# One RWKV step on Trainium2: the decay in a step's last operation, outputs behind the next step's first products, row halves in turn

## The chip, the cores and the metric

The kernel runs on one core of a Trainium2 chip. The core has a matrix engine (PE, which reads its stationary operand by a weight load, PEld), a vector engine (DVE), a scalar engine (ACT), a general engine (POOL) and a queue that issues transfers (SP); each works through its own instructions in order and waits for the others by semaphores. The metric is the device time of one execution in microseconds (us), as the median of several runs.

## The reference, cut to what matters

One layer of a hybrid network for 512 latent tokens and 128 context tokens, all float32:

```python
proj = (x * (1 + sc1) + sh1) @ p["w_in"]              # one input projection
att = _attend(q_nope, q_rope, k_nope, k_rope, v)      # 8 heads, low-rank keys and values
rw, s_fwd, s_bwd = _rwkv_mixer(proj[..., OFF_RW:], ...)  # 16 heads x 64, one scan per direction
x = _post_norm(x, g1, _merge(att, rw, p), ...)        # output projection, norm
x = _post_norm(x, g2, _swiglu(x * (1 + sc2) + sh2, p), ...)   # feed-forward part

def step(S, inp):                                     # the RWKV scan, token by token
    r_t, w_t, k_t, v_t, kk_t, a_t = inp
    sa = jnp.einsum("bhvk,bhk->bhv", S, -kk_t)
    S = S * w_t[:, :, None, :] + sa[..., None] * (kk_t * a_t)[:, :, None, :] + v_t[..., None] * k_t[:, :, None, :]
    return S, jnp.einsum("bhvk,bhk->bhv", S, r_t)
```

The scan runs forwards and backwards over the tokens; `w_t` is the decay of the state.

## The kernel before, in words

The first 1540 us hold three jobs. The **main** job multiplies the modulated input with 33 tiles of `w_in` (each 16 x 6 products of 320 columns, written `acc<-xh,whi` and the like in the profile: a float32 product is split into three of a faster type). The **RWKV** job goes through 8 pairs of heads. The **attention** job follows once the main job is done. From 1540 us on come the output projection and the feed-forward part, with one product after the other from streamed weights; the change leaves these lines alone.

RWKV takes the tokens in chunks of 64, so a pair has two halves (`j`), each with five steps (`e`) in both directions at once. A half has these stages, each a generator that gives way with `yield HOP[...]`:

- `rwkv_decays`: four small products with `lw` (128 rows), each corrected by one over 64 rows (`m<-xl,lw`), then the decays `ld`, `D` and `dc`.
- `rwkv_prep` and `rwkv_grams`: 20 products `m<-pr,nk` with 64 rows each, for the two heads of the pair in the two halves of the rows; their masks are put on while they are taken from PSUM into `pr`, `mab` and `mrb`.
- `inverse`: `mab` is brought into another layout (`nd`), a triangular solve runs on DVE, and its result `tc` goes back to PE (`m<-tc,mab`). Beside it `rwkv_turned` turns the values (`sv`, `zv`) and `nk` (`bk`).
- `rwkv_chain`: the five steps, one behind the other. A step is: the first product `m<-sv,pr`, copied to `xs`; the solve `m<-xs,uf`, copied to `zv`; the update `m<-zv,bk`, from which the next state `sv` is made with the decay `dc`; and the outputs `m<-pr,sv` plus `m<-mrb,zv`, added into `y`.

The order on PE is written out when the program is built. `Jobs` keeps a clock of PE (`Tensor.now`, raised by a cost per product) and always takes the job of the best rank that is ready; RWKV has the best rank, the main and the attention job the last. A job that gives way is ready again after the time it yields (`HOP`, with one table for the stretch beside the main job and one beside attention). So these numbers say how much other work PE is given between two products that depend on each other; at run time PE waits if the data are not there. The other engines' order is made by a scheduler.

The last stretch of the main job is set by `fs`: the tiles 2 to 25 belong to the pairs 0 to 7, three each, 26 to 29 are the queries, 30 and 31 the keys and values, 32 the rotary key; a pair's RWKV begins when its three tiles are there.

PSUM has three banks for small results (`mps`, the tile `m`) and two double banks (`acc`). In attention, `kslot` gives out 12 buffers: four hold the compressed keys and values all along, two the rotary key (`krh`, `krl`), the others keys and values of the heads in turn. The lower part of the rotary key is multiplied for one head of a pair in one half of the rows (`acc<-krl,qx`, 64 rows).

Of the kernel before, what the change touches and what calls it, by code (L numbers as in the profile page):

```python
# [15 lines left out]
P = 128  # L16
# [11 lines left out]
C = 64  # L28
# [18 lines left out]
for _n, _w in (("ident", 128), ("gmask", 128), ("lmask", 32), ("par", 2), ("blk", 128), ("cen", 128), ("blk2", 2), ("sel", 2),  # L47
# [22 lines left out]
HOPS = ({"load": 3.73, "pow": 3.84, "kk": 1.18, "dec": 0.92, "prep": 1.68, "vr": 2.17, "tv": 0.36, "bk": 0.36, "gram": 0.36,  # L70
         "inv": 14.4, "d32": 1.2, "d32b": 1.92, "d64": 1.44, "d64b": 1.44, "x": 0.48, "s": 0.6, "y": 0.0, "p": 1.06,
# [3 lines left out]
         "inv": 16.13, "d32": 1.51, "d32b": 1.96, "d64": 1.3, "d64b": 1.44, "x": 0.61, "s": 0.6, "y": 0.0, "p": 1.08,  # L75
# [20 lines left out]
class Tensor:  # L96
# [5 lines left out]
    def matmul(self, out, lhsT, rhs, start, stop):  # L102
# [8 lines left out]
        self.now += t / 2400.0  # L111
# [46 lines left out]
def step_kernel(ctx: ExitStack, tc: tile.TileContext, a: dict, o: dict, upto: int = 99, npairs: int = NPAIR, dbg=None):  # L158
# [397 lines left out]
    def inverse(mab):  # L556
# [5 lines left out]
        for b in range(4):  # L562
            pr = slice(32 * b, 32 * b + 32)
            co = 32 * (b % 2)
            A.copy(nd[pr, :].rearrange("p (t c q) -> p c q t", c=16, q=2)[:, :NCH],  # L565
                   mab[pr, :, co: co + 32].rearrange("p c (q t) -> p c q t", q=2))
# [143 lines left out]
    def rwkv_decays(i, j, sh):  # L710
# [3 lines left out]
        for d in range(2):  # L714
            col = 8 * d + i
            for t, c0, x, r_, b in ((ld, 0, xw, slice(0, 64), w0_h), (ta, 256, xa, slice(64, 128), a0_h)):
                ps = mps()
                w = lw[:, c0 + d * P: c0 + d * P + P]
# [4 lines left out]
                yield HOP["dec"]  # L723
# [43 lines left out]
    def rwkv_turned(i, j, sh, u):  # L767
# [6 lines left out]
        for d in range(2):  # L774
# [6 lines left out]
            for h in range(2):  # L781
                A.copy(sv_[hrow(h), es, h, :], ch(ps[hrow(h), :HN]))
                V.tensor_copy(zv[hrow(h), es, h, :], ch(ps[hrow(h), :HN]))
# [8 lines left out]
    def rwkv_grams(u):  # L792
# [3 lines left out]
        for e0, n in EG:  # L796
            es = slice(e0, e0 + n)
            for h in range(2):
                ps = mps()
# [9 lines left out]
                tt(V, mrb[rows(h), es], ps4[rows(h), :, 1, :],  # L809
                   con("gmask")[rows(h), C:].unsqueeze(1).broadcast_to([C, n, C]), ALU.mult)  # L810
                yield HOP["gram"]
# [7 lines left out]
    def rwkv_chain(i, j, sh, u):  # L819
# [23 lines left out]
        def outputs(c):  # L843

            ps = mps()
            for d in range(2):
                e = 5 * d + c
                ms = slice(0, C) if d == 0 else slice(None, None, -1)
                for h in range(2):
                    T.matmul(ps[rows(h), cc(d)], sv_[:, e, h, :], pr[h][:, e, 1, :][:, ms], start=True, stop=False)  # L850
                for h in range(2):
                    T.matmul(ps[rows(h), cc(d)], zv[rows(h), e, h, :], mrb[rows(h), e, :][:, ms], start=False, stop=True)
            for d in range(2):
                yc = y[:, nat(d, j)][:, cc(c if d == 0 else 4 - c)]
                if j == 0:
                    A.copy(yc, ps[:, cc(d)])
                else:
                    tt(V, yc, ps[:, cc(d)], yc, ALU.add)

        for e in range(5):  # L860
# [6 lines left out]
            yield HOP["x"]  # L867
# [7 lines left out]
            to = [AFTER[j, d][e] for d in range(2)]  # L875
            ds = [d for d in range(2) if to[d]]
# [4 lines left out]
            sd = rtile("sd", 2 * C, "xs", 2)  # L881
            n = len(ds)
            for h in range(2):
                rh = rows(h)
                es = slice(5 * ds[0] + e, 5 * ds[-1] + e + 1, 5)
                dv = slice(ds[0] * C, ds[-1] * C + C)
                s2 = sd[rh, dv].rearrange("p (d v) -> p d v", v=C)
                tt(V, s2, pn[rh, dv].rearrange("p (d v) -> p d v", v=C), sv_[rh, es, h, :], ALU.add)
# [1123 lines left out]
```

## Time and profile before

| | |
|---|---|
| median of three runs | 3558.94 us (3550.21 to 3559.14) |
| the profiled execution | 3555.39 us, of which its span 3553.6 us |
| busy share of the span | PE 95%, PEld 85%, DVE 73%, ACT 41%, POOL 28% |
| first RWKV products (`m<-pr,nk`) | 264 us |
| last state written (`out_states`) | 1524 us |
| first product of the output projection | 1555 us |
| mean granted PE clock | 0.963 |

A row of the timeline has start, duration, engine, line, operation, tiles and shape, and how many equal ones were merged (x8); in brackets how long the engine sat idle before and what released it. A product in float32 is two instructions on PE, one in the faster type is one. A row of the groups has busy time and mean duration of one, then the idle time before. Durations of PE overlap, since it is pipelined; how long PE is taken up by a row is read from the start of the row after it.

### The profile page before, as it was taken

The page shows a single profiled execution, that of the slowest core. Times are in us where ns is not written, and L with a number is a line of the kernel's source. Part 1 is how long each engine was busy: PE and PEld are TensorE (multiplying, and loading weights), DVE is VectorE, ACT ScalarE, POOL GpSimd, SP SyncE. Part 2 cuts the span into 40 slices and gives each one's busy share as a digit, 9 for nine tenths or more (in the row PEclk, how much of TensorE's full clock was granted, in tenths as well). Part 3 has the DMA queues.
Part 4 walks back from the last instruction along what each step waited for, and adds up shares of the span by engine and source line. Part 5 has one row for each costly group of instructions (what it writes and reads, how often), then busy time and mean ns, then how long its engine had stood idle before and what let it go on. Part 6 is the DMA issues. An engine that isn't in the chain of part 4 may idle for free.

```text
span 3553.6 us, 71134 instructions
## 1 busy us (share of the span) xinstructions
PE 3376.3 (95%) x27538; PEld 3022.9 (85%) x27538; DVE 2609.0 (73%) x4721; ACT 1459.1 (41%) x2987; POOL 992.5 (28%) x944
## 2 busy tenths in 40 slices
PE   8979999999999899999979999999999999999987
PEld 4667776777887678889979999999999999899886
DVE  1355676666676877667788888888888879778798
ACT  1143333433444444444554444444444444334334
POOL 0021111111111212112164444344444442122245
PEclk9988999999999999999989999999999999999997
DMA  8753444444212111066534543444434468766743
GB/s 299 236 172 120 148 150 134 157 146 144 65 58 77 50 38 37 21 203 189 164 116 131 164 134 128 140 133 128 134 128 141 133 231 288 268 238 222 244 138 106
DMA packets 289715, 529.04 MB, mean 149 GB/s; under 512 B 31008, under 2 KB 83680, under 8 KB 289376
## 3 DMA queue, kind: packets, MB, share of 16 engines
q1 hardware_dynamic: 289376, 524.49, 45.1%
q8 instruction: 216, 3.54, 0.4%
q14 instruction: 123, 1.01, 0.1%
HBM read 429.65 MB, written 93.09 MB: 147 GB/s over the span
## 4 chain that ended last, share of the span: by engine, by line
PE 55%; DVE 6%; issue 2%; DMA 2%; ACT 1%; POOL 1%; SPq 0%; ACTq 0%; DVEq 0%; POOLq 0%
PE b L112 47%; PE acc L112 3%; PE m L112 3%; DVE ql L226 1%; DMA op<-hd 1%; PE x L112 1%; DVE z L226 1%; POOL z L226 1%; PE acc L116 0%; DMA raw<-in_w_down_dram 0%; DVE z L235 0%; DVE ns L226 0%; DVE raw L226 0%; ACT nd L565 0%; DVE u L226 0%
## 5 line engine op out<-in xcount | busy, mean ns | idle before, releaser
L226 DVE TENSOR_TENSOR ql<-raw,qh 128x512 fp32r<-128x512 f32 (+1 forms) x1136 | 926.3, 830 | 263.5 <-ACT qh L1290 242.8
L1290 ACT CAST qh<-raw 128x512 fp32r<-128x512 f32 (+1 forms) x1136 | 661.1, 588 | 914.0 <-PE b L112 784.1
L226 POOL TENSOR_TENSOR raw<-raw,raw 128x512 f32<-128x512 f32 (+1 forms) x288 | 397.0, 1380 | 852.2 <-DVE ql L226 654.4
L112 PE MATMUL b<-t,qh 128*128 128x320 f32 x2816 | 622.7, 310 | 8.2 <-ACT qh L1290 7.1
L112 PE MATMUL b<-op,qh 128*128 128x320 f32 x2464 | 547.0, 315 | 18.3 <-DMA op<-hd 18.0
L112 PEld LDWEIGHTS b<-t,qh 128*128 128x128 f32 x2816 | 472.6, 189 | 9.6 <-ACT qh L1290 8.1
L112 PE MATMUL b<-p,qh 128*128 128x320 f32 x2112 | 468.4, 311 | 0.0
L112 PE MATMUL b<-t,ql 128*128 128x320 f32 x1408 | 435.8, 310 | 5.8 <-DVE ql L226 5.8
L112 PEld LDWEIGHTS b<-op,qh 128*128 128x128 f32 x2464 | 418.2, 192 | 24.3 <-issue 11.7
L112 PE MATMUL b<-op,ql 128*128 128x320 f32 x1232 | 375.2, 317 | 19.7 <-DVE ql L226 19.5
L112 PEld LDWEIGHTS b<-p,qh 128*128 128x128 f32 x2112 | 355.8, 189 | 0.1
L112 PE MATMUL b<-p,ql 128*128 128x320 f32 x1056 | 328.9, 312 | 8.0 <-DVE ql L226 8.0
L112 PEld LDWEIGHTS b<-t,ql 128*128 128x128 f32 x1408 | 264.9, 188 | 8.0 <-DVE ql L226 8.0
L112 PEld LDWEIGHTS b<-op,ql 128*128 128x128 f32 x1232 | 233.1, 192 | 27.5 <-DVE ql L226 27.2
L112 PE MATMUL acc<-xh,whi 128*128 128x320 f32 x928 | 239.8, 341 | 0.3 <-DVE vS L1145 0.2
L112 PE MATMUL acc<-xl,whi 128*128 128x320 f32 x928 | 237.3, 338 | 0.0
L112 PE MATMUL b<-mh,qh 128*128 128x320 f32 x1024 | 231.0, 315 | 6.2 <-ACT qh L1290 6.1
L112 PE MATMUL acc<-xh,wlo 128*128 128x320 f32 x928 | 235.6, 336 | 0.8 <-DVE wlo L226 0.8
L226 DVE TENSOR_TENSOR raw<-raw,raw 128x512 f32<-128x512 f32 (+1 forms) x288 | 216.5, 764 | 12.5 <-POOL raw L226 10.6
L112 PEld LDWEIGHTS b<-p,ql 128*128 128x128 f32 x1056 | 199.6, 189 | 10.6 <-DVE ql L226 10.6
L263 ACT CAST whi<-raw 128x512 fp32r<-128x512 f32 (+1 forms) x156 | 94.8, 608 | 255.9 <-PE acc L112 167.1
L226 DVE TENSOR_TENSOR wlo<-raw,whi 128x512 fp32r<-128x512 f32 (+1 forms) x156 | 107.3, 688 | 110.5 <-ACT whi L263 78.5
(328 smaller groups left out, 5853.0 us busy)
## 6 DMA issues: line engine op xcount, KB each, us to landing
wm<-in_w_mod_dram SPq DMA_DIRECT2D x64, 1024.0 KB, 5.5
op<-hd SPq DMA_DIRECT2D x154, 320.0 KB, 5.8
raw<-in_w_gate_dram SPq DMA_DIRECT2D x188, 256.0 KB, 2.7
raw<-in_w_up_dram SPq DMA_DIRECT2D x188, 256.0 KB, 2.9
raw<-in_w_down_dram SPq DMA_DIRECT2D x224, 192.0 KB, 2.8
raw<-in_w_in_dram SPq DMA_DIRECT2D x132, 256.0 KB, 2.7
wm<-in_w_mod_dram SPq DMA_DIRECT2D x64, 512.0 KB, 6.1
raw<-in_w_out_dram SPq DMA_DIRECT2D x128, 256.0 KB, 3.0
```

Of the source, the lines that this page charges most:

```text
L112: self.eng.matmul(out, lhsT, rhs, start=start, stop=stop)
L226: eng.tensor_tensor(out=out, in0=x, in1=y, op=op)
L263: A.copy(hi, r)
L1290: A.copy(hi, x)
```

## The change

Several edits, all in the first 1540 us:

- `rwkv_chain`: the state times its decay (`sd`) is worked out by POOL at the step's begin, and the step's last operation on DVE is one that multiplies the update from PSUM with the decay and adds `sd` (64 x 64, one for each head and direction). The outputs of a step are issued behind the first product of the next step, without giving way between them and the solve; both directions have a PSUM bank of their own, and products of one shape stand together.
- `rwkv_grams`: the products of the two heads alternate; `mrb` is copied by ACT and masked by one DVE operation at the end.
- `rwkv_decays`: the two full products first, then the two over 64 rows.
- `rwkv_turned`: the copies of `zv` by ACT in place of DVE. `inverse`: two of the four copies to `nd` by DVE in place of ACT.
- `krl` becomes two buffers of 128 rows, each with zeros in the other head's half.
- The tiles 23 to 25 go ahead of 30 to 32. The costs of alternating products (`share`) and several waits in `HOPS` are new numbers.

```diff
-"gram": 0.36, "inv": 14.4, ... "s": 0.6, "y": 0.0, "p": 1.06,          (beside the main job)
+"gram": 0.75, "inv": 12.0, ... "s": 0.72, "p": 0.72,
-"gram": 0.79, "inv": 16.13, ... "s": 0.6, "y": 0.0, "p": 1.08,         (beside attention)
+"gram": 0.79, "inv": 14.0, ... "s": 0.72, "p": 0.72,
...
-        fs = list(range(2 + N_PART, ATT_POS)) + list(range(26, 33)) + list(range(ATT_POS, 26))
+        fs = list(range(2 + N_PART, ATT_POS)) + list(range(26, 30)) + list(range(ATT_POS, 26)) + list(range(30, 33))
...
-            A.copy(nd[pr, :].rearrange("p (t c q) -> p c q t", c=16, q=2)[:, :NCH],
+            (V.tensor_copy if b % 2 else A.copy)(nd[pr, :].rearrange("p (t c q) -> p c q t", c=16, q=2)[:, :NCH],
...
+            for t, w, x, r_, b, ps in both:
                 T.matmul(ps[:, :HN], w, x[:, nat(d, j)], start=True, stop=False)
-                T.matmul(ps[:, :HN], w[r_], xl[r_, nat(d, j)], start=False, stop=True)
+            for t, w, x, r_, b, ps in both:
+                T.matmul(ps[:, :HN], w[r_], xl[r_, nat(d, j)], start=False, stop=True, share=0.5)
...
-                V.tensor_copy(zv[hrow(h), es, h, :], ch(ps[hrow(h), :HN]))
+                A.copy(zv[hrow(h), es, h, :], ch(ps[hrow(h), :HN]))
...
-            for h in range(2):
-                ps = mps()
-                for e in range(n):
+            both = [mps(), mps()]
+            for e in range(n):
+                for h, ps in enumerate(both):
                     T.matmul(ps[:, e * P: e * P + P], nk[rows(h), e0 + e].rearrange("p b t -> p (b t)"),
-                             pr[h][rows(h), e0 + e].rearrange("p b t -> p (b t)"), start=True, stop=True)
+                             pr[h][rows(h), e0 + e].rearrange("p b t -> p (b t)"), start=True, stop=True, share=0.5)
...
-                tt(V, mrb[rows(h), es], ps4[rows(h), :, 1, :],
-                   con("gmask")[rows(h), C:].unsqueeze(1).broadcast_to([C, n, C]), ALU.mult)
+                A.copy(mrb[rows(h), es], ps4[rows(h), :, 1, :])
+        tt(V, mrb, mrb, con("gmask")[:, C:].unsqueeze(1).broadcast_to([P, NCH, C]), ALU.mult)
...
             A.copy(xs, px[:, :2 * C])
-            yield HOP["x"]
+            sd = rtile("sd", 2 * C, "xs", 2)
+            for h in range(2):
+                tt(G, sd[rh, dv].rearrange("p (d v) -> p d v", v=C), sv_[rh, es, h, :],
+                   dc[rh, es].unsqueeze(2).broadcast_to([C, n, C]), ALU.mult)
+            if e:
+                outputs(e - 1)
+            else:
+                yield HOP["x"]
...
-                tt(V, s2, pn[rh, dv].rearrange("p (d v) -> p d v", v=C), sv_[rh, es, h, :], ALU.add)
-                    tt(V, dst, s2, dcb, ALU.mult)
+                for d in ds:
+                    stt(dst, pn[rh, cc(d)], dc[rh, q: q + 1], sd[rh, cc(d)], ALU.mult, ALU.add)
-            yield HOP["y"]
-            outputs(e)
-            yield HOP["p"] if e < 4 else 0.0
+            if e < 4:
+                yield HOP["p"]
+        outputs(4)
...
-        krh, krl = kslot("krh", F32R), kslot("krl", F32R)
+        krl = [kslot("krl", F32R) for _ in range(2)]
+        for h in range(2):
+            G.memset(krl[h][rows(1 - h)].bitcast(F32), 0.0)
+            tt(V, krl[h][rows(h)], krs[rows(h)], krh[rows(h)].bitcast(F32), ALU.subtract)
...
-                            (qx[:, qs], krh[:, ks], 3), (qx[rr, qs], krl[rr, ks], 4)):
+                            (qx[:, qs], krh[:, ks], 3), (qx[:, qs], krl[hd % 2][:, ks], 4)):
```

What the change makes of the order on PE, at three places. First the grams of one half of the fourth pair; `acc` is the main job's work between them. Before, one head's products, four at a time, then main work, then the other head's:

```order
L112 MATMUL acc_8017<-xh_1025,wlo_8106 128x320 x2
L112 MATMUL m_8293<-pr_8256,nk_8255 128x128 x4
L112 MATMUL acc_8017<-xh_1346,whi_8197 128x320 x2
L112 MATMUL acc_8017<-xl_1347,whi_8197 128x320 x2
L112 MATMUL m_8311<-pr_8257,nk_8255 128x128 x4
L112 MATMUL acc_8017<-xh_1346,wlo_8198 128x320 x2
```

Now:

```order
L113 MATMUL acc_8061<-xl_283,whi_7906 128x320 x2
L113 MATMUL m_8132<-pr_8098,nk_8097 128x128
L113 MATMUL m_8133<-pr_8099,nk_8097 128x128
L113 MATMUL m_8132<-pr_8098,nk_8097 128x128
L113 MATMUL m_8133<-pr_8099,nk_8097 128x128
...
L113 MATMUL acc_8061<-xh_282,wlo_7907 128x320 x2
```

The heads (`pr_8098` and `pr_8099`) alternate, each with a bank of its own, eight products in one block.

Second, a step of the chain in the second half of the first pair. Before, update, outputs of both directions one after the other, main work, and then the next step's first product:

```order
L112 MATMUL m_3644<-xs_3632,uf_166 64x64 x4
L112 MATMUL acc_3391<-xh_998,wlo_3553 128x320 x2
...
L112 MATMUL m_3657<-zv_3145,bk_3146 64x64 x4
L112 MATMUL m_3667<-pr_2986,sv_3144 64x64
L112 MATMUL m_3667<-pr_2987,sv_3144 64x64
L112 MATMUL m_3667<-mrb_3019,zv_3145 64x64 x2
...
L112 MATMUL x_3234<-wm_621_3583,cs 32x512 x4
L112 MATMUL acc_3391<-xh_1007,wlo_3553 128x320 x2
L112 MATMUL m_3686<-sv_3144,pr_2986 64x64
```

Now (a step of the same half; the outputs are those of the step before):

```order
L113 MATMUL m_3578<-zv_3138,bk_3139 64x64 x4
L113 MATMUL acc_3501<-xl_292,whi_3357 128x320 x2
L113 MATMUL acc_3501<-xh_291,wlo_3358 128x320 x2
L113 MATMUL acc_3501<-xh_650,whi_3502 128x320 x2
L113 MATMUL m_3599<-sv_3137,pr_2947 64x64
...
L113 MATMUL m_3609<-pr_2947,sv_3137 64x64
...
L113 MATMUL m_3609<-mrb_2980,zv_3138 64x64 x2
L113 MATMUL m_3610<-mrb_2980,zv_3138 64x64 x2
L113 MATMUL m_3621<-xs_3604,uf_166 64x64 x4
```

Between the update and the next first product stand six products of main work and nothing else; the outputs have moved behind it, up against the solve.

Third, the end of the stretch. Before, the last RWKV products (`sg`) are among the last five rows ahead of the output projection (`b<-mh`):

```order
L112 MATMUL m_16813<-sg_16719,gw_16716 128x320
L116 MATMUL acc_16817<-cst,P_16725 128x128 x5
L112 MATMUL m_16825<-sg_16719,gw_16716 128x320
L112 MATMUL m_16828<-pp_16737,vS_15867 128x128
L112 MATMUL x_16747<-PT_16816,vS_15867 128x128 x5
...
L112 MATMUL b_17208<-mh_17098,qh_17187 128x320 x2
```

Now they stand among the keys of the fifth head:

```order
L113 MATMUL m_16140<-sg_16033,gw_16030 128x320
L113 MATMUL acc_16117<-ch_13451,whi_16067 128x384 x2
L113 MATMUL acc_16117<-cl_13452,whi_16067 128x384 x2
L113 MATMUL m_16147<-sg_16033,gw_16030 128x320
L113 MATMUL acc_16117<-ch_13451,wlo_16068 128x384 x2
L113 MATMUL acc_16157<-kh_15477,qh_15454 128x320
```

Behind them come 342 rows of attention alone, with 17 of the 32 blocks of scores, before the first `b<-mh`. Behind that product the order of PE is the same for some 10,800 rows; but for a handful of swaps, only in the last norm do instructions of the engines change places.

More of the change, by code (lines that the diff above doesn't have):

```diff
@@ L100, in __init__, with matmul @@
         self.eng, self.now = eng, 0.0
-    def matmul(self, out, lhsT, rhs, start, stop):
+    def matmul(self, out, lhsT, rhs, start, stop, share=1.0):
         n = 1
@@ L110, in matmul @@
             t = 4 * max(n, 16) * (0.25 if m <= 32 and n > 64 else 0.7 if m <= 32 else 0.8 if m <= 64 else 1.0)
-        self.now += t / 2400.0
+        self.now += share * t / 2400.0
         self.eng.matmul(out, lhsT, rhs, start=start, stop=stop)
@@ L843, in outputs @@
         def outputs(c):
[L845 to L848, printed above, removed]
+            pss = [mps()[:, :C] for _ in range(2)]
+            ms = (slice(0, C), slice(None, None, -1))
+            for d, ps in enumerate(pss):
                 for h in range(2):
-                    T.matmul(ps[rows(h), cc(d)], sv_[:, e, h, :], pr[h][:, e, 1, :][:, ms], start=True, stop=False)
+                    T.matmul(ps[rows(h)], sv_[:, 5 * d + c, h, :], pr[h][:, 5 * d + c, 1, :][:, ms[d]], start=True, stop=False)
+            for d, ps in enumerate(pss):
                 for h in range(2):
-                    T.matmul(ps[rows(h), cc(d)], zv[rows(h), e, h, :], mrb[rows(h), e, :][:, ms], start=False, stop=True)
+                    T.matmul(ps[rows(h)], zv[rows(h), 5 * d + c, h, :], mrb[rows(h), 5 * d + c, :][:, ms[d]], start=False, stop=True)
             for d in range(2):
```

51 lines of the change are left out of this document (22 added, 29 removed).

## The prediction

> **What bounds the kernel now.** I first read the page's chain of waits, which runs over PE for more than half of the span, and then the busy times by stage. The columns of the stage view are: stage, length, PE, PEld, DVE, ACT and POOL busy, granted PE clock, share of the transfer engines, GB/s.
>
> ```profile
> 300.00:1150.00 850.00, 813.38 (x9360) 643.15 (x9358) 563.56 (x1267) 317.18 (x768) 128.86 (x195) 0.95 0.38 121
> 1150.00:1540.00 390.00, 367.71 (x3897) 297.42 (x3896) 271.30 (x634) 178.16 (x429) 75.00 (x92) 0.98 0.13 38
> 1540.00:3554.00 2014.00, 1930.95 (x12808) 1900.03 (x12808) 1651.85 (x2584) 882.79 (x1630) 763.54 (x600) 0.97 0.52 172
> ```
>
> Of the 1240 us in which the change works, PE is busy for 1181 (95%), DVE for 835 (67%), ACT for 495 (40%), POOL for 204 (16%). PE works through one fixed list, so the stretch lasts as long as its list plus the waits in it, and RWKV's latencies count only where the list has too little other work between two dependent products. So I ask two things of each edit: what time on PE's list it takes away, and what wait it uncovers. The last 2014 us keep their list and I leave them as they are.
>
> **The grams.** Rows of PE's timeline (start, then the duration of the merged row); I read the start-to-start distance:
>
> ```profile
> 806.71 1.16 PE L112 MATMUL m<-pr,nk 64*128 64x128 f32 x8
> 807.80 0.56 PE L112 MATMUL acc<-xh,whi 128*128 128x320 f32 x2
> ...
> 814.40 0.71 PE L112 MATMUL m<-pr,nk 64*128 64x128 f32 x4
> 815.04 0.56 PE L112 MATMUL acc<-xh,whi 128*128 128x320 f32 x2
> ```
>
> Eight instructions take 1.09 us and four 0.64, so one costs 0.1125 and a block another 0.19 for the change of shape. Sixteen halves have four blocks of eight and two of four each: 64 x 1.09 + 32 x 0.64 = 90.2 us. Now a half has two blocks of sixteen and one of eight. All of one head's products lie in one half of the rows, and the trace never shows the two row halves in turn. What it shows is columns in turn:
>
> ```profile
> 1532.52 1.31 PE L112 MATMUL m<-cst,rt 128*64 128x128 f32 x20
> ...
> 1533.76 0.81 PE L112 MATMUL m<-sg,gw 128*128 128x320 f32 x2
> ```
>
> Twenty instructions over the same 128 columns of data in 1.24 us, 0.062 each: two column halves run side by side. If row halves do too, sixteen instructions take the time of eight: 32 x 1.09 + 16 x 0.64 = 45.1 us, **45 us less**. If they don't: 32 x 1.99 + 16 x 1.09 = 81.1, 9 us less. I take the first, since the row it is nearest to is also two halves of the array in turn, and keep 9 as the other end. The Trainium skill, "TensorE: Matmul & The Clock Gate", section "Part 3: Packing small matmuls — row/col tiling", says that products in different row groups run concurrently, and "TensorEngine Tiling (Array Packing)", "Gotcha 1: PSUM Pressure", that two row tiles must not write to one PSUM bank at a time, which the two banks heed. By that rule the first end holds; no run here shows it yet.
>
> **The rotary key and the decays.** The rows of one block of scores, and of one decay:
>
> ```profile
> 1404.93 0.31 PE L112 MATMUL acc<-kh,ql 128*128 128x320 f32 x1
> 1405.08 0.31 PE L112 MATMUL acc<-krh,qx 128*128 128x320 f32 x1
> 1405.31 0.41 PE L112 MATMUL acc<-krl,qx 64*128 64x320 f32 x1
> 1405.65 0.38 PE L112 MATMUL m<-kh,qh 128*128 128x256 f32 x1
> ```
>
> ```profile
> 459.78 0.41 PE L112 MATMUL m<-xw,lw 128*128 128x320 f32 x1
> 460.13 0.41 PE L112 MATMUL m<-xl,lw 64*128 64x320 f32 x1
> 460.46 0.56 PE L112 MATMUL acc<-xh,wlo 128*128 128x320 f32 x2
> ```
>
> A product in the full shape takes 0.15 us. The one ahead of `krl` takes 0.23 and `krl` itself 0.34, so the 64 rows cost 0.27 us more than 128 would. With 64 blocks' halves and 8 prompts: 72 x 0.27 = **20 us less**. The zeros are written once. A pair of decays costs 2 x (0.35 + 0.33) = 1.36 us; with the full ones together and the two halves of rows side by side 0.15 + 0.35 + 0.33 = 0.83; 32 pairs, **17 us less**, or 9 if the halves run one after the other.
>
> **The step.** One step, PE and DVE (`sd`, `sv`):
>
> ```profile
> 404.28 0.45 PE L112 MATMUL m<-zv,bk 128*64 128x64 f32 x8
> 404.56 0.29 PE L112 MATMUL m<-pr,sv 128*64 128x64 f32 x4
> 404.78 0.33 PE L112 MATMUL m<-mrb,zv 64*64 64x64 f32 x4
> 404.78 0.61 DVE L226 TENSOR_TENSOR sd<-m,sv 64x128 f32<-64x128 f32 x2 [0.87 <-PE m L112]
> 405.04 0.34 PE L112 MATMUL m<-pr,sv 128*64 128x64 f32 x4
> 405.30 0.33 PE L112 MATMUL m<-mrb,zv 64*64 64x64 f32 x4
> 405.42 0.60 DVE L226 TENSOR_TENSOR sv<-sd,dc 64x128 f32<-64x128 f32 x2
> 405.57 0.56 PE L112 MATMUL acc<-xh,wlo 128*128 128x320 f32 x2
> ...
> 406.56 0.45 PE L112 MATMUL acc<-xh,wlo 128*128 128x320 f32 x2
> 406.94 0.45 PE L112 MATMUL m<-sv,pr 128*64 128x64 f32 x8
> 407.32 0.56 PE L112 MATMUL acc<-xh,whi 128*128 128x320 f32 x2
> ```
>
> Two main products take 0.30 us, and 0.38 where the shape changes behind them; a change costs some 0.09. A step had nine changes (into and out of the first product, the solve and the update with its outputs, and three among the outputs). Now it has five. 64 steps x 4 x 0.09 = **23 us less**.
>
> The wait it uncovers: from the update to the next first product PE had 2.66 us (404.28 to 406.94), 1.29 of it the update with the outputs, and the state was ready at 406.02, so 0.9 us were to spare. With the outputs gone from there, the list has 0.28 for the update, six main products (0.9) and a change: 1.3 us. The state needs 0.50 until DVE begins, then four operations on 64 x 64, by the groups:
>
> ```profile
> L226 DVE TENSOR_TENSOR sd<-m,sv 64x64 f32<-64x64 f32 x32 | 7.1, 222 | 10.6 <-PE m L112 10.1
> ```
>
> 4 x 0.22 = 0.9, and 0.1 to hand over: 1.5. PE comes 0.25 us early, 64 times: **16 us more**. And since nothing is to spare now, another operation in DVE's queue (0.7 us where it is a weight's lower part) is no longer hidden; if one step in four is hit by 0.6, **10 us more**. If the fused operation costs nothing beyond one of the old ones, the ends are 0 and 26.
>
> POOL's share of the step (two multiplications of 64 x 128) has all of the first product, the outputs, the solve and the update to hide behind, about 2.9 us; the nearest row is `pr` below, 0.96 for 320 columns, so two end within 1.9. I cost it at nothing; what happens without that cover is the third rival.
>
> ```profile
> 425.36 1.26 POOL L226 TENSOR_TENSOR t<-u 128x641 f32<-128x641 f32 x1 [37.24 <-ACT zv L872]
> 426.57 3.83 POOL L226 TENSOR_TENSOR pr<-r,D 64x320 f32<-64x320 f32 x4
> 428.77 1.71 DVE L226 TENSOR_TENSOR fs<-sd,dc 64x64 f32<-64x64 f32 x2
> ```
>
> **The inverse and the ends.**
>
> ```profile
> 444.38 0.49 DVE L783 COPY zv<-m 64x320 f32<-64x320 f32 x1
> ...
> 457.26 0.49 DVE L599 STREAM_TRANSPOSE tc<-uc 128x320 f32<-128x320 f32 x1
> ...
> 458.97 0.89 PE L112 MATMUL m<-tc,mab 32*32 32x32 f32 x80
> ```
>
> The solve's result was there 1.2 us before PE asked for it. DVE loses four such copies of `zv` among the solve's operations (2.0 us) and gains the mask of `mrb` (some 0.8, from operations of its width). The planned wait falls by 2.4 (2.1 beside attention). Left over: 1.2 + 2.0 - 0.8 - 2.4 = 0; a half loses 0 to 1 us, I take 0.5: **8 us more**. The copies that go to ACT lie on an engine busy for 40%. The tiles 30 to 32 now end the main job, so attention's first loads stand in SP's queue behind the store of tile 32, once: **5 us more**. At the end 17 blocks of attention run without RWKV to fill PE:
>
> ```profile
> 1522.36 0.82 DVE L1152 TENSOR_REDUCE smx<-acc 128x1 f32<-128x640 f32 x1 [0.52 <-PE acc L112]
> ...
> 1524.63 0.80 POOL L232 TENSOR_SCALAR P<-P,smx 128x640 f32<-128x640 f32 x1 [5.08 <-DVE smx L1154]
> ```
>
> From scores to weights 3.1 us pass, and PE works two blocks ahead (over 6 us), but one more buffer of twelve is taken by `krl`; I put 0.4 us on a block: **7 us more**.
>
> **Sum.** 45 + 20 + 17 + 23 = 105 us off PE's list, 16 + 10 + 8 + 5 + 7 = 46 us of new waits: 59 us less. The profiled execution took 3555.4 us (1.8 of them outside its span), 3.5 less than the median shown: 3555.4 - 59 = **3496 us**.
>
> **The rivals.**
>
> *The waits don't appear*: work already in the queues covers them. For it, the state's price may be lower than four rows say; against it, the list's 1.3 us. 3555 - 105 = 3450.
>
> *Row halves don't run side by side*: the list loses 9 + 20 + 9 + 23 = 61. For it, the trace shows no such pair; against it, the column halves. 3555 - 61 + 46 = 3540.
>
> *POOL comes into the step* (slower). Each step's last operation waits for `sd`, which stands in POOL's queue, in 15 of 80 steps directly behind an operation as long as `t` (1.26) or `ks`. Also, `fs` above took 0.86 each beside POOL's `pr`, where its shortest took 0.21: operations of DVE that read two tiles from SBUF are slowed while POOL works. The Trainium skill, "GPSIMD Engine Reference", section "8. Key points", warns of just this contention; the row agrees, 0.86 against 0.21. Against it, the new operation reads PSUM, and `sd` has about 1 us to spare. From 0.7 us a step on (80 steps, 58 us) the gain is gone; at 1.3 us, the length of `t`, it is 104 us: 3496 + 104 = 3600.
>
> *Attention alone is bound by its softmax*: 17 blocks wait 2 us each rather than 0.4: 3496 + 27 = 3523.
>
> **How the numbers follow.** The forecast with its own spread (3470 to 3515) has 0.53, no new waits 0.12, row halves in turn without gain 0.16, softmax 0.09, POOL 0.10. The predicted time is 3496. A measurement can tell about 0.3% here, 11 us. Faster: 0.53 + 0.12 + 0.09 and half of the second rival (15 us less, close to the bound), 0.08, and a little of POOL's, 0.02: 0.84. Same: the other 0.06 of the second and 0.02 of POOL's: 0.08. Slower: 0.08. The range leaves out half of the first rival and most of POOL's: 3452 to 3548.
>
> **What would show it.** Right: alternating grams 1.1 us for sixteen instructions; `krl` 0.15 apart; the first product of a step waiting for DVE's last operation by some tenths of a microsecond; the last state written near 1380 us and attention behind it with PE over 85% busy; the later part as long as before. Wrong: sixteen grams in 2 us; PE or DVE waiting for POOL's `sd`; long waits of PE, with a lower granted clock, where attention runs alone; a later part that changes by more than 10 us.

## The result, and the profile after

The changed kernel takes 3490.8 us (median of four, 3488.8 to 3500.3) against 3556.0 before (median of four runs, one more than in the table ahead of the prediction): a ratio of 0.983, 95% interval 0.9814 to 0.9847, which is 54 to 66 us less, and 65 by the two medians. The prediction had 59 less and 3496. The sum came out close, in part by luck: several of its terms were far off, in opposite directions. The profiled execution after took 3500.3, the longest of the four, against 3555.4 before, so sums from the two profiles come to 55 us.

The busy times by stage of the kernel after, cut where RWKV ends and where the output projection begins, and then of the kernel before, cut at the same place of its program (columns as in the prediction):

```profile
300.00:1150.00 850.00, 783.53 (x10111) 633.08 (x10104) 571.76 (x1279) 366.74 (x954) 205.05 (x343) 0.96 0.37 123
1150.00:1390.00 240.00, 198.85 (x2441) 169.72 (x2440) 163.55 (x370) 108.84 (x270) 54.96 (x80) 0.92 0.13 41
1390.00:1490.00 100.00, 88.51 (x648) 84.00 (x647) 40.97 (x88) 41.74 (x97) 16.59 (x23) 0.98 0.13 40
1490.00:3498.00 2008.00, 1929.16 (x12808) 1896.64 (x12808) 1651.17 (x2583) 880.61 (x1627) 767.46 (x600) 0.98 0.52 172
```

```profile
1546.00:3554.00 2008.00, 1930.61 (x12808) 1899.68 (x12807) 1651.00 (x2583) 881.16 (x1626) 763.54 (x600) 0.97 0.52 172
```

The later part is as long as before, 2008 us. All of the gain lies ahead of the output projection, whose first product starts at 1490.0 instead of 1545.7 (the table ahead of the prediction has 1555 for it; the trace of the kernel before has `b<-mh` from 1545.7 on). From 300 to 1150 us PE gets through 751 instructions more (10,111 against 9360), and yet it is busy for less time, 92% against 96%. Attention alone takes the last 100 us, with PE busy for 88%.

To split this I took the distance from each PE instruction's start to the next one's, gave every kind of neighbours (shape, shape of the one behind, and whether it is a product's first or second instruction) its median over the run as its place on the **list**, and put the rest, the **waits**, on the instruction that came late. Up to the output projection:

| us | before | after | measured | prediction |
|---|---|---|---|---|
| list in all | 1322.0 | 1227.2 | -95 | -105 |
| grams | 80.3 | 40.5 | -40 | -45 |
| rotary key (`krl`, `krh` ahead of it) | 39.6 | 20.8 | -19 | -20 |
| decays (`xw`, `xl`) | 29.4 | 17.2 | -12 | -17 |
| step (`sv,pr`, `zv,bk`, `pr,sv`, `mrb`) | 113.1 | 91.2 | -22 | -23 |
| waits in all | 216.4 | 255.2 | +39 | +46 |
| step (ahead of its first product, solve, update and outputs) | 49.8 | 32.0 | -18 | +26 |
| grams | 27.3 | 45.9 | +19 | 0 |
| second product of the decays (`xa`) | 0.6 | 15.3 | +15 | 0 |
| the solve's result (`tc,mab`) | 3.6 | 17.0 | +13 | +8 |
| all others | 135.2 | 145.0 | +10 | +12 |

Three cautions on this table. Its rows move by some 2 or 3 us when the kinds of neighbours are drawn a little differently, but the two totals move more: drawn by the run of one tile, the same traces give 81 us less of list and 25 more of waits. Only their difference, 56 us, is measured as it stands. Second, a wait here also holds what a lowered clock costs: PE was granted half its clock for 157 us ahead of the output projection, in both kernels alike, so that it cancels between them (a block of eight grams took 2.00 us at 267 us in the kernel before, where most took 1.09). Third, for the grams a median mixes blocks with and without a stop. Block by block, sixteen instructions without a stop take 1.09 us and eight 0.65, 45 us over all halves, against 90 before: the list lost the 45 that were forecast, and what stands beside it grew from 8 to 33 us.

The rows that the prediction asked for. Sixteen alternating grams, and the rotary key, in PE's timeline of the kernel after:

```profile
404.53 1.16 PE L113 MATMUL m<-pr,nk 64*128 64x128 f32 x16
405.62 1.05 PE L113 MATMUL x<-cst,ev 128*128 128x2 f32 x8
```

```profile
1441.01 0.30 PE L113 MATMUL acc<-krh,qx 128*128 128x320 f32 x1
1441.15 0.31 PE L113 MATMUL acc<-krl,qx 128*128 128x320 f32 x1
1441.29 0.31 PE L113 MATMUL acc<-kh,qh 128*128 128x320 f32 x1
```

Sixteen in 1.09 us, where eight took 1.09 before; `krl` 0.14 apart, where it took 0.34. The groups of PE from 300 to 1540 us, before and after (busy time, mean ns of one, then the idle time of PE ahead of them and what ended it):

```profile
L112 PE MATMUL m<-pr,nk 64*128 64x128 f32 x600 | 93.9, 294 | 0.0
L112 PE MATMUL m<-zv,bk 128*64 128x64 f32 x576 | 39.4, 239 | 14.9 <-DVE zv L873 10.5 <-ACT zv L872 4.5
L112 PE MATMUL m<-sv,pr 128*64 128x64 f32 x640 | 37.6, 240 | 0.4 <-DVE sv L226 0.4
L112 PE MATMUL m<-xa,lw 128*128 128x320 f32 x28 | 11.5, 410 | 0.2 <-DVE y L226 0.2
```

```profile
L113 PE MATMUL m<-pr,nk 64*128 64x128 f32 x600 | 55.9, 294 | 20.2 <-DVE y L227 9.0 <-POOL sv L846 8.3 <-ACT mrb L815 2.9
L113 PE MATMUL m<-sv,pr 128*64 128x64 f32 x640 | 40.7, 240 | 1.0 <-DVE sv L236 0.8
L113 PE MATMUL m<-zv,bk 128*64 128x64 f32 x576 | 37.4, 237 | 5.0 <-DVE zv L895 5.0
L113 PE MATMUL m<-tc,mab 32*32 32x32 f32 x1239 | 15.7, 206 | 11.2 <-DVE tc L600 11.1
L113 PE MATMUL m<-xa,lw 128*128 128x320 f32 x28 | 10.8, 387 | 10.6 <-DVE y L227 10.6
```

A step's first product (`m<-sv,pr`) waits 1.0 us in all, where the prediction put 26. By these rows, which count only time in which PE is idle, the waits now stand in front of the grams and of `m<-xa,lw`, where from 300 us on there was next to none.

### The profile page after: what moved, and what is told of

The parts are those of the page before. It is cut to its first block, busy times and chain, and to the rows that moved or that the text cites. A ratio compares the mean times of both kernels' runs of the same rounds, so it can differ in the third digit from the quotient of the medians.

```text
span 3498.5 us, 71287 instructions
## 1 busy us (share of the span) xinstructions
PE 3255.5 (93%) x27538; PEld 2961.4 (85%) x27538; DVE 2555.3 (73%) x4562; ACT 1480.9 (42%) x3115; POOL 1070.4 (31%) x1106
## 5 line engine op out<-in xcount | busy, mean ns | idle before, releaser
L227 POOL TENSOR_TENSOR raw<-raw,raw 128x512 f32<-128x512 f32 (+1 forms) x288 | 394.4, 1371 | 849.6 <-DVE ql L227 662.2
L113 PEld LDWEIGHTS b<-mh,qh 128*128 128x128 f32 x1024 | 175.4, 192 | 7.6 <-ACT qh L1302 6.8
```

The costliest lines, as they stand in the source:

```text
L113: self.eng.matmul(out, lhsT, rhs, start=start, stop=stop)
L227: eng.tensor_tensor(out=out, in0=x, in1=y, op=op)
```

## The experiments

Each experiment is compared with the changed kernel's 3490.8; the ratios are to the kernel before, with their 95% intervals. The kernel before was run beside each of them, with medians from 3553.1 to 3558.7, so some 5 us of a difference between two medians can come from there. Two kernels whose intervals overlap I take as not told apart by the times, and say so where the trace tells more.

| | median us | ratio | interval |
|---|---|---|---|
| the change | 3490.8 | 0.983 | 0.9814 to 0.9847 |
| e1 heads apart | 3489.1 | 0.981 | 0.9784 to 0.9834 |
| e2 rotary key on 64 rows | 3509.9 | 0.987 | 0.9844 to 0.9895 |
| e3 outputs back | 3527.5 | 0.993 | 0.9902 to 0.9949 |
| e4 state in two operations | 3514.1 | 0.988 | 0.9855 to 0.9912 |
| e4b decay on DVE | 3507.9 | 0.986 | 0.9842 to 0.9887 |
| e5 longer wait ahead of the grams | 3466.1 | 0.975 | 0.9720 to 0.9770 |
| e7 e5, and ahead of the gate | 3462.5 | 0.974 | 0.9721 to 0.9763 |
| e8 tiles in the old order | 3493.1 | 0.982 | 0.9797 to 0.9842 |
| e9 copies back | 3527.7 | 0.992 | 0.9898 to 0.9944 |
| e10 alternating at full cost | 3486.9 | 0.980 | 0.9769 to 0.9832 |
| e12 e7, and `zv` on ACT | 3450.4 | 0.970 | 0.9683 to 0.9718 |
| e13 e5 with the heads apart | 3472.1 | 0.976 | 0.9747 to 0.9777 |

### e1: the heads apart

```diff
-            for e in range(n):
-                for h, ps in enumerate(both):
-                    T.matmul(ps[...], nk[...], pr[h][...], ..., share=0.5)
+            for h, ps in enumerate(both):
+                for e in range(n):
+                    T.matmul(ps[...], nk[...], pr[h][...], ...)
```

> The changed kernel, but in each block of grams the products of the first head stand ahead of those of the second, without the half cost; all else as in the change. By the forecast's term the alternation is worth 45 us, and a block of sixteen gives no new wait: 3491 + 45 = 3536. The rival reading of the trace of the change: the alternation takes 40 us off PE's list, but a block whose second product belongs to the other head waits some 1.4 us more in each half, for the second head's operand and for the second PSUM bank; with the first head's eight products ahead (1 us) most of that wait is covered again, so only 3491 + 40 - 15 = 3516. Below 3505 both are wrong on the concurrency.

3489.1, not slower at all: below the bound at which the expectation called both readings wrong. The timeline of e1 in three places: a block of sixteen, eight instructions of the one head and then eight of the other; and two blocks of eight, four and four; each with what follows it:

```profile
740.95 1.71 PE L113 MATMUL m<-pr,nk 64*128 64x128 f32 x16
742.58 1.05 PE L113 MATMUL x<-cst,ev 128*128 128x2 f32 x8
...
745.43 1.18 PE L113 MATMUL m<-pr,nk 64*128 64x128 f32 x8
746.54 0.56 PE L113 MATMUL acc<-xh,wlo 128*128 128x320 f32 x2
...
811.92 0.72 PE L113 MATMUL m<-pr,nk 64*128 64x128 f32 x8
812.57 0.56 PE L113 MATMUL acc<-xh,whi 128*128 128x320 f32 x2
```

Sixteen take 1.63 us, not 2.0, and eight take 0.65 in 12 of the 16 halves, no more than when the heads alternate. The block at 745.43, with 1.11, is the only one in which the two heads hardly overlap without a stop in it. So PE runs a part of the one head beside the other in the blocks of sixteen, and all of it in most blocks of eight, though the program doesn't alternate. Over all halves the blocks of grams come to 90 us from start to start in e1, 78 in the change and 98 before, waits included. In the change 20 us of the 40 saved are lost again at once. And e1 does not lose the 12 us between them: its other waits are shorter, 9.8 less in front of `m<-tc,mab` and 8.8 less in front of `x<-cst,ev`. The heads apart were counted in full, so the planner had also laid the rest of the list otherwise. Two things had to be separated, the wait in the block and the count.

### e5 and e10: the wait, and the count

The first block of a half in the change:

```profile
744.33 0.48 PE L113 MATMUL m<-pr,nk 64*128 64x128 f32 x2
745.96 1.13 PE L113 MATMUL m<-pr,nk 64*128 64x128 f32 x14 [1.14 <-POOL sv L846]
```

PE does the first head's first product and then stands, since the next one belongs to the other head. In 13 of 16 halves (all but the first and the last two) it stops there for 1.2 to 2.0 us. Where the half is a pair's second, the `pr<-kk,D` of DVE that makes the second head's operand ends 0.15 us before PE goes on; where it is a pair's first, DVE's last `y<-m,y`, which empties a bank of the outputs, ends some 0.02 us before. The row names POOL's `sv`, which ended in between, but no gram reads it; that it is DVE is what I infer from the program and these times.

```diff
-"prep": 1.68,       (e5, beside the main job)
+"prep": 3.2,
-... pr[h][...], start=True, stop=True, share=0.5)       (e10)
+... pr[h][...], start=True, stop=True)
```

> The changed kernel with one number changed: the planned wait between the preparation of a half and its grams, beside the main job, from 1.68 to 3.2 us. In the trace of the change PE stops after the second product of the first block of grams in 14 of 16 halves, 1.2 to 2 us each, for the second head's operand or for a PSUM bank that DVE has yet to empty; about 20 us. Theory: PE gets main work for that time and the stop is gone, 3491 - 20 = 3471. Rival: a half lasts longer by the same 1.5 us and what PE does meanwhile lacks later, so 3491 or a little more.

> The changed kernel, grams alternating as in the change, but counted by the planner at full cost rather than half (one number). The kernel with the heads apart (e1) was not slower than the changed one though its blocks take some 12 us more of PE. Theory: e1 won that back since the planner, which counted its grams in full, gave out less main work too early and laid the list otherwise; then the alternating grams at full cost come to 3489 - 12 = 3477 or thereabouts. Rival: alternating itself costs something elsewhere (both heads' banks are emptied together and late), and this kernel stays at 3491.

e5 comes to 3466.1, 25 us less. The same place in its timeline:

```profile
743.59 1.16 PE L113 MATMUL m<-pr,nk 64*128 64x128 f32 x16
744.68 0.56 PE L113 MATMUL acc<-xh,wlo 128*128 128x320 f32 x2
```

```profile
L113 PE MATMUL m<-pr,nk 64*128 64x128 f32 x600 | 54.7, 295 | 13.1 <-ACT mrb L815 12.2 <-DVE pr L227 0.7
L113 PE MATMUL m<-zv,bk 128*64 128x64 f32 x576 | 38.7, 239 | 16.9 <-DVE zv L895 16.0 <-ACT zv L894 0.9
```

The stop in the first block is gone (that block sums to 23 us over the halves, from 44). Part of it stands now in front of the later blocks, which wait for ACT to empty the banks of the first (`mrb`, 12.2 us). The wait could be filled because a half's length does not set the end: RWKV ended 100 us ahead of attention in the change, and in e5 the last state's store was issued at 1372 us, against 1373 in the change.

The 25 us are what the number brought, but not shown to be this stop alone. All blocks of grams together fell only from 78 to 71 us, 7 of the 34 us between the two profiled executions. Two other waits fell by 8 us each (in front of `m<-tc,mab` from 17.0 to 9.3, of `x<-cst,ev` from 9.6 to 1.1), the one in front of the update grew by 13, and PE stood at half its clock for 127 us instead of 157, which is worth up to 15. Why PE stood there for less time was not tested.

e10, 3486.9, differs neither from the change nor from e1. The count alone is not shown to matter. In its trace, though, the two waits that were shorter in e1 are short as well (9.8 and 0.9 us): they go with how the list is laid out, and not with the heads being apart.

### e13: alternating alone

```diff
 (e5, and)
-            for e in range(n):
-                for h, ps in enumerate(both):
+            for h, ps in enumerate(both):
+                for e in range(n):
```

> e5 (the changed kernel with 3.2 us planned ahead of the grams) with the products of the two heads apart, and counted at the same half cost, so that the planner's clock and all else of PE's list stay as in e5. The price of alternating alone, with its wait gone. Forecast: two blocks of sixteen at 0.9 us and one of eight at 0.45 us more in each half, 16 x 2.25 = 36 us: 3466 + 36 = 3502. Rival, from the traces of e1: PE runs ahead in the other half of the rows by itself when the first half's products queue up, so of blocks side by side without alternating only half or less is lost: 3466 + 8 to 18 = 3474 to 3484.

3472.1, 6 us more than e5, and the intervals overlap; even their far ends are only 20 us apart. The forecast's 36 us for alternating are refuted. The first block of a half in e13, and its group:

```profile
747.81 1.71 PE L113 MATMUL m<-pr,nk 64*128 64x128 f32 x16
749.45 0.56 PE L113 MATMUL acc<-xh,wlo 128*128 128x320 f32 x2
```

```profile
L113 PE MATMUL m<-pr,nk 64*128 64x128 f32 x600 | 66.5, 290 | 2.0 <-ACT mrb L814 1.9
```

Eight instructions of one head and eight of the other, one head behind the other in the program, take 1.64 us, not 2.0: after about four instructions in one half of the rows, records come in pairs a few ns apart, which I read as PE running the second head beside the rest of the first (the records don't name the head). In the blocks of eight they come in pairs from the first on, and take 0.65 us, as they do alternating. What is left, 0.55 us for a block of sixteen, alternating gives back, but then the next block waits for the banks: 13.1 us of idle time in e5 against 2.0 here. All blocks together take 71 us in both.

### e2: the rotary key

```diff
-        krl = [kslot("krl", F32R) for _ in range(2)]
+        krl = kslot("krl", F32R)
...
-    (qx[:, qs], krl[hd % 2][:, ks], 4)
+    (qx[rr, qs], krl[rr, ks], 4)
```

> The changed kernel with the one rotary buffer of 64 rows back; it also has one buffer more for the keys of the heads. Forecast and trace of the change agree: 72 products at 0.27 us, so 3491 + 19 = 3510. The rival: the buffer that the two copies take makes the keys of the next head late, and 64 rows give it back, then less than 3505.

3509.9, 19 more: the size of the forecast's term, and no price shows for the buffer that the second copy takes. By the ratios it is 14, and the two intervals just touch; but all four times of e2 (3506.1 to 3512.6) lie above the longest of the change, and in its trace the list of the two rotary products is 20 us longer.

### e3, e4 and e4b: the step

```diff
-            if e:                                  (e3: outputs behind the update again)
-                outputs(e - 1)
-            else:
-                yield HOP["x"]
+            yield HOP["x"]
...
-            if e < 4:
-                yield HOP["p"]
-        outputs(4)
+            outputs(e)
+            yield 1.07 if e < 4 else 0.0
```

```diff
-                    stt(dst, pn[rh, cc(d)], dc[rh, q: q + 1], sd[rh, cc(d)], ALU.mult, ALU.add)   (e4; POOL's sd goes too)
+                tt(V, s2, pn[...], sv_[rh, es, h, :], ALU.add)
+                tt(V, dst, s2, dcb, ALU.mult)
```

```diff
-                tt(G, sd[...], sv_[rh, es, h, :], ...)         (e4b)
+                tt(V, sd[...], sv_[rh, es, h, :], ...)
```

> The changed kernel with the outputs of a step back behind its update (one bank for both directions, the old order, the old wait of about 1.07 behind them and the old gap before the solve); the fused last operation stays. The forecast put the new place at 23 us of shape changes less and 16 + 10 us of waits more for the state, so nearly nothing: 3491 - 3 = 3488. The rival, from the trace of the change: the shape changes are saved, and the first product starts as soon as the first of the four parts of the state is there, so the waits never came; taking the outputs back then costs the 22 us of the list and some of the waits of the old step: 3491 + 22 to 30 = 3513 to 3521.

> The changed kernel with the old way of the state: an addition and a multiplication on DVE for each row half instead of four fused operations, no work of POOL in the step; places and planned waits as in the change. The forecast has four operations of 0.22 until the state is whole, the old way has two of 0.29 and two of 0.29 (1.16 us): about the same, 0.25 us more at each of 64 steps at most, 3491 + 0 to 16. The rival, that the first product needs only the first part of the state: this part is there after 0.28 us in the fused way and after 0.58 in the old one, and the whole after 1.0 against 1.16; with some 0.1 us to spare now the old way costs 0.2 to 0.3 us a step, 3491 + 13 to 19 = 3504 to 3510. If POOL's work in the step had a price (the third rival of the prediction), this kernel would be faster than the changed one.

> The changed kernel with the state times its decay (sd) worked out by DVE instead of POOL, at the same place of the program. The rival of the prediction in which POOL costs the step 0.7 us and more: then this kernel is faster than the changed one, below 3480. The forecast (POOL's work is free, DVE's is not): two operations of 0.29 on DVE at each of 80 steps, 46 us of DVE in all; beside the solve they have some 2.9 us to lie in, so most is covered, but the copies back on DVE (e9) cost 37 us for about 65 us of DVE, so by that proportion 26: 3491 + 10 to 30.

e3: 3527.5, 37 more, where the forecast's terms had 3 less. The list grows by the 22 us of the shape changes. The waits in front of the step's products grow by 17, while the grams and `tc` wait 19 less in the profiled execution. Why the new place has no wait for the state, a step of the kernel after shows:

```profile
451.55 0.45 PE L113 MATMUL m<-zv,bk 128*64 128x64 f32 x8
...
452.30 0.99 DVE L236 SCALAR_TENSOR_TENSOR sv<-m,dc,sd 64x64 f32<-64x64 f32 x4
...
453.01 0.60 PE L113 MATMUL m<-sv,pr 128*64 128x64 f32 x7
```

DVE's four operations end at 453.29, and PE starts the first product at 453.01: each product needs one of the four parts only, and PE follows DVE part by part. e4 agrees: with the two operations over both directions the first part is whole later, and it takes 3514.1, 23 more, with the list unchanged and 18 us more of waits in front of the first product, 9.6 of them time in which PE is idle, against 1.0 in the change:

```profile
L113 PE MATMUL m<-sv,pr 128*64 128x64 f32 x640 | 49.0, 242 | 9.6 <-DVE sv L227 7.1 <-DVE fs L227 0.8
```

It does not separate the first part from the whole state, which also comes later (1.24 us behind DVE's start in e4's trace, 0.99 in the change), and its profiled execution, the longest of its four, had PE at half its clock for 194 us, against 157.

e4b: 3507.9, 17 more by the medians and 12 by the ratios, whose intervals touch. It is not faster, as it would be if POOL's `sd` (0.52 us each) cost the step more than DVE's time does. That POOL doesn't slow the step is read from the trace of the change: of the 47.1 us that DVE is idle ahead of a step's last operation, which needs `sd`, PE ends 44.7, and POOL's `sd` is not among what it waited for.

```profile
L236 DVE SCALAR_TENSOR_TENSOR sv<-m,dc,sd 64x64 f32<-64x64 f32 x224 | 55.5, 281 | 47.1 <-PE m L113 44.7
```

### e8 and e9: the tiles' order, and the copies

```diff
-        fs = ... + list(range(26, 30)) + list(range(ATT_POS, 26)) + list(range(30, 33))     (e8)
+        fs = ... + list(range(26, 33)) + list(range(ATT_POS, 26))
```

```diff
-                A.copy(zv[hrow(h), es, h, :], ch(ps[hrow(h), :HN]))      (e9)
+                V.tensor_copy(zv[hrow(h), es, h, :], ch(ps[hrow(h), :HN]))
...
-            (V.tensor_copy if b % 2 else A.copy)(nd[...], ...)
+            A.copy(nd[...], ...)
...
-                A.copy(mrb[rows(h), es], ps4[rows(h), :, 1, :])
+                tt(V, mrb[rows(h), es], ps4[rows(h), :, 1, :], con("gmask")..., ALU.mult)
```

> The changed kernel with the tiles of the last pair behind those of the keys and values, as before. The forecast gave the new order only costs: 5 us for the store in SP's queue, 7 us for attention running alone; so 3491 - 12 = 3479. The rival: with the old order RWKV ends last, its waits without enough work of attention to fill them, and the wait at the start of attention (9 us for the inverse, 5 for the rotary key in the trace of the change) only moves: 3491 + 5 to 20.

> The changed kernel with the copies of zv on DVE again, all four copies to nd on ACT and the masks of mrb taken on DVE while they leave PSUM, with the shorter planned wait for the inverse as it is. Theory: DVE has some 2 us more among the solve's operations of a half, so PE waits for the solve: 16 halves of 0.8 to 1.5 us, 3491 + 13 to 24. Rival: DVE's idle time takes them in, 3491 within 5.

e8: 3493.1, no difference; neither the 12 us of costs nor a gain shows. In e8, too, the last state's store is issued at 1371 us and attention runs alone behind it, so it is not the tiles' order that ends RWKV early (before, that store was issued at 1524), and e8 could not take the cost of attention alone away. The long wait at the start of attention (9 us in front of `m<-tc,mab`, near 1170 us in the change) is there in both orders: 15.4 and 17.0 us of waits in front of all `tc`.

e9: 3527.7, 37 more. PE's list is the same to 0.5 us, the waits grow by 31, spread over many rows. The two largest in the groups of e9:

```profile
L113 PE MATMUL m<-tc,mab 32*32 32x32 f32 x1280 | 17.8, 218 | 20.4 <-DVE tc L600 20.4
L113 PE MATMUL m<-xa,lw 128*128 128x320 f32 x28 | 11.2, 400 | 15.2 <-DVE y L227 15.2
```

Both are ended by DVE. Up to the output projection DVE is busy for 943 us in e9 against 904 in the change: 39 us more of DVE go with 37 us more of time (the 65 us in the expectation of e4b were too many). Part of it may be the clock: PE stood at half of it for 189 us on the way there, against 157, worth up to 16 us. Which of the three kinds of copies does it was not told apart.

### e7 and e12: further than the change

```diff
-"pow2": 3.84, "gup0": 0.0,        (e7: e5, and)
+"pow2": 3.84, "gup0": 2.2,
...
-            V.tensor_copy(lanes(zv, 1, e), lane2(psg, 1))      (e12: e7, and)
+            A.copy(lanes(zv, 1, e), lane2(psg, 1))
...
-"s": 0.72,
+"s": 0.96,
```

> e5 with a second number changed: the planned wait ahead of the last two products of a pair's end (with the gate, m<-sg,gw), beside the main job, from 0 to 2.2 us. In the change and in e5 the decays behind them stop for 1 to 3.6 us between their first and second product, since the second PSUM bank is emptied only when POOL's y<-y,ks is done; some 12 us in all in the change, 8 to 10 in e5 beside the main job. Theory: 3466 - 8 = 3458. Rival: another of the stops takes its place, 3466 within 4.

> e7 with both copies of a step's solve (zv) on ACT instead of one on ACT and one on DVE, and a planned wait of 0.96 instead of 0.72 us for them. In e5 the update stops 1 to 3 us in one step of most halves, since DVE's copy stands behind preparations of the next half; the excess in front of the update is 24.5 us there against 11.8 in the change. Theory: that excess falls to a few us: 15 us less than e7, about 3443. Rival: ACT's two copies one behind the other (0.26 each) come later than the plan in every step, 80 x 0.1 to 0.3: no gain or up to 10 us more than e7.

The place that e7 is for, in the kernel after:

```profile
562.68 0.31 PE L113 MATMUL m<-xw,lw 128*128 128x320 f32 x1
564.97 0.41 PE L113 MATMUL m<-xa,lw 128*128 128x320 f32 x1 [1.99 <-DVE y L227]
```

In e7 the idle time in front of `m<-xa,lw` falls from 9.7 to 2.1 us, but that in front of the update rises from 16.9 to 22.3. 3462.5, which is not to be told from e5: the rival. In e12 that wait, for DVE's copy of `zv`, is gone, and a smaller one for the state has come:

```profile
L113 PE MATMUL m<-sv,pr 128*64 128x64 f32 x640 | 42.6, 239 | 13.8 <-DVE sv L236 13.7
L113 PE MATMUL m<-zv,bk 128*64 128x64 f32 x576 | 35.5, 240 | 0.7 <-ACT zv L894 0.7
```

3450.4, a ratio of 0.970 (0.9683 to 0.9718): 12 us less than e7 and 40 less than the changed kernel. It is the fastest version here.

## Why the prediction was right, step by step

- **What bounds the kernel** (PE's list, and what it waits for): right. The later part did not move, and less list and more waits (95 and 39 us by the table, 81 and 25 by another grouping) give the 56 us by which the output projection starts earlier.
- **Grams, 45 us**: the list lost 40 by the table and 45 by the blocks without a stop, as the side-by-side end had it. The step that failed is the sentence that sixteen instructions cost 45 us less by alternating and nothing else. No wait was put on the block, though the second head's operand and the second bank now stood ahead of its second product: 19 us came back there by the table, 24 by the blocks. Before and after, the blocks cost 98 and 78 us with their waits, so 20. And with a longer planned wait alternating is not needed for it: in e13, with the heads in one block and not alternating, the blocks took the same 71 us as in e5, nearly without stops. The prediction also overlooked a row that it shows: in `m<-mrb,zv` (64*64) the two heads lie in different halves of the rows, and of the columns too, and four instructions took 0.26 us, so the trace before did have row halves in turn.
- **Rotary key, 20 us**: right (19 by the list and by e2).
- **Decays, 17 us**: 12 on the list, but 15 of waits in front of `m<-xa,lw`, which now needs its bank at once with the first product's, while DVE's `y<-y,m` behind POOL's `y<-y,ks` still holds it. By these two the edit won nothing. No kernel undid it alone, so that stays an account of the trace.
- **Shape changes of the step, 23 us**: right, 22.
- **The wait for the state, 16 + 10 us**: the step that failed most. "PE comes 0.25 us early, 64 times" took the state as one thing that is ready when the fourth operation ends. PE needs one part for each product; the wait grew by 3 us in all. And the waits ahead of the update fell by 11 and those ahead of the outputs by 9, which I had not counted. Moving the outputs is worth 37 us (e3), not -3.
- **The fused operation, copies and masks**: I gave the first no gain of its own and let the others cancel against a shorter planned wait. Put back, they cost 23 us (e4) and 37 us (e9). The rows that show it are the waits ended by DVE; a part of both, up to 18 and 16 us in the profiled executions, can be the longer time at half clock.
- **The inverse, 8 us**: 13, of which 9 are one wait at the start of attention.
- **Start of attention 5, attention alone 7**: e8 shows no difference between the two orders, so the first isn't seen. The last 100 us went as forecast: the last state's store was issued at 1373 us, PE over 88% busy at a clock of 0.98, so the softmax rival falls; no run measures the 7 us by themselves.
- **The rivals**: row halves do run side by side; POOL is not in the step (DVE's last operation didn't wait for `sd`); the waits did appear, but elsewhere.

So the size was right, and by luck as far as the waits go: 46 us of them were forecast and 25 to 39 came, by the grouping, of which the largest, in front of the grams and the decays, were not among those named, while the largest that was named, 26 us for the state, came to 3. The parts undone one at a time add up to more than the 65 us of the medians (19, 37, 23 and 37), perhaps because the planned waits were left as in the change; they are what each part is worth beside the others, not shares of a sum. What also stays open is how much of each difference is the chance place of single waits of 5 to 9 us: e1 lost 12 us of blocks against the change and had them back from two such places.

## What to carry to other kernels

When products of two independent streams are put into one block, ask for each operand and each PSUM bank when it is ready: a block waits for the latest of them, and what the packing saves can be lost at the first product of the second stream. A wait for several results is not a wait for the last one where the consumer takes them one by one. And where a latency-bound job ends well ahead of the rest, a longer planned wait can be the better one: the 1.5 us more in e5 won 25 us.

## What the runs showed of the hardware

- Products in the two halves of PE's rows run side by side without alternating in the program. Sixteen instructions took 1.64 us in e13, against 1.09 alternating and 2 x 1.09 for two separate blocks of eight; eight took 0.65 us, alternating or not.
- PE ran at half its clock for part of the way to the output projection: 127 us in e5, 157 before and in the change, 189 in e9, 194 in e4. A block of eight grams took 2.00 us in such a stretch, against 1.09. What sets it is not shown here.
- A fused operation of DVE on 64 x 64, the update from PSUM, took 0.28 us each in the group, but the four of a step started some 0.23 apart (0.99 for four); POOL's product of 64 x 128 took 0.52, where I had bounded it by 0.96 for 320 columns.
